# A stick-breaking scan that reads its factors from PSUM, and a planner that knows of a shared port

## The chip, the cores and the metric

The kernel runs on one core of a Trainium2 chip. Its time is the device time of one launch in microseconds (us); the median of three runs is given. Five engines work on it at once, each in its own order: TensorE (PE, with its weight loads PEld), VectorE (DVE), ScalarE (ACT), GpSimd (POOL) and SyncE (SP), which issues the DMAs. The program divides PSUM, into which PE writes its products, into eight banks of 512 fp32 columns.

## The reference

One decoder layer in fp32, 2048 tokens of width 1024. A combined projection feeds two head groups of eight heads: latent attention with softmax (MLA), and stick-breaking attention. Both outputs are normalised, concatenated and projected; a SwiGLU feed-forward network follows. The change is in the second group:

```python
z = jnp.einsum("bhqd,bhkd->bhqk", qb, kf) * scale
strict = k_pos[None, :] < q_pos[:, None]
log_beta = jax.nn.log_sigmoid(z)
log_one_minus = jnp.where(strict, jax.nn.log_sigmoid(-z), 0.0)
suffix = lax.cumsum(log_one_minus, axis=3, reverse=True) - log_one_minus
a = jnp.where(strict, jnp.exp(log_beta + suffix), 0.0)
o = jnp.einsum("bhqk,bhkd->bhqd", a, vf)
```

So the weight of key s is beta[s] times the product of 1 - beta over the keys between s and the query.

## The kernel before

**Precision.** Operands of large products are split into a high part in fp32r and the rest, a low part (`split_w` line 518, `split_ps` line 509): ACT writes the high part (`whi`, `ph`), DVE subtracts it (`wlo`, `pl`), and PE makes three products out of them (`mm3`).

**Stages.** `ORDER` (line 86) lists, for four blocks of 512 tokens, the projection P, the attention A, and the feed-forward parts F. All of their instructions go into one `Plan`. Attention runs from about 200 to 1900 us, beside projections and the first feed-forward products; afterwards PE has dense products alone.

**Attention.** For each head, block and stretch of 1024 keys there is a `Unit`; `step` (line 754) makes four rows of 128 queries. `sb_row` (line 636) cuts the keys into pieces of up to 512, last piece first. For each piece PE makes the scores in a PSUM tile `ps_s` (two products), ACT writes 1 - beta into an SBUF tile `nb` and beta into `p` (line 647), and DVE scans `nb` backwards into `tb` (lines 657 to 665): each step multiplies the running value with the next factor. A masked scan of 128 columns comes first in the piece on the diagonal. POOL then multiplies p by tb (line 666). The value that the scan ends with starts the next piece. `mix` (line 585) takes pairs of rows: PE transposes p into a PSUM tile `pt`, ACT and DVE split it into `ph` and `pl`, and PE multiplies v with both into `ot`.

**Buffers.** The PSUM banks are shared: two for scores (`S_B`), two for transposes (`TP_B`), one for `ot` (`O_B`), the rest for dense accumulators (`ps_gu`, `ps_d`, `ps_o` and others). In SBUF there are two `nb` and two `tb` (`NT_BUFS`), and six p (`P_BUFS`).

**What sets the order.** `Plan.order` (line 282) is a list scheduler that runs while the program is built. Each instruction has a cost (`price`, line 237), each pair of engines a handover (`HOP`), and each pool its buffers. At each moment an engine takes the ready instruction of lowest rank, then of lowest index. What comes out is each engine's fixed order; on the chip an engine executes strictly in it and waits where an operand is late. A product into `ot` needs the one recorded before it on the same columns. `issue` (line 436) writes all instructions, so they all carry line 450 in the profile.

Of the kernel before, what the change touches and what calls it, by code (L numbers as in the profile page):

```python
# [12 lines left out]
F32 = mybir.dt.float32  # L13
F32R = mybir.dt.float32r
I32 = mybir.dt.int32
AF = mybir.ActivationFunctionType
ALU = mybir.AluOpType
# [4 lines left out]
P = 128  # L22
# [37 lines left out]
NT_BUFS = 2  # L60
SWAP_SPAN = 0.5
AHEAD = 10
RT_BUFS = 3
SLACK = 0.0
DMA_ISSUE = 500.0
DMA_RATE = 300.0
DMA_DONE = 910.0
# [114 lines left out]
class Plan:  # L182
# [21 lines left out]
    def record(self, engine, method, args, kwargs):  # L204
        t = Task()
        t.engine, t.method, t.args, t.kwargs = engine, method, args, kwargs
        t.index, t.key = len(self.tasks), (self.rank, len(self.tasks))
        views = [(i, a) for i, a in enumerate(args)] + list(kwargs.items())
        views = [(k, v) for k, v in views if isinstance(v, View)]
        first = 0 if "out" not in kwargs else "out"  # L210
        t.out = next((v for k, v in views if k == first), None)
        t.needs, t.then, t.bases = set(), [], []
        for k, v in views:
            write = k in (first, "accum_out")
            base, region = v.base, v.region or v.base.whole
            if base not in t.bases:
                t.bases.append(base)
            for old, oreg, owrite in base.seen:
                if k == first and engine == "tensor" == old.engine and kwargs.get("start"):
                    t.needs.add(old.index)  # L220
                if (write or owrite) and old is not t and all(a < d and c < b for (a, b), (c, d) in zip(region, oreg)):
                    t.needs.add(old.index)
            if write:
                base.seen = [s for s in base.seen if s[0] is t or not all(a <= c and d <= b for (a, b), (c, d) in
                                                                           zip(region, s[1]))]
            base.seen.append((t, region, write))
        for b in t.bases:
            b.uses += 1
        t.table, t.cost, t.tail = self.price(t)
        if engine != "tensor" and any(b.pool.managed and b.pool.psum for b in t.bases):  # L230
            boost = ACC_FIRST if any(b.tag == "acc" for b in t.bases) else ATT_FIRST
            t.key = (self.rank - boost, t.index)
        elif engine != "tensor" and self.dense:
            t.key = (self.rank - DENSE_FIRST, t.index)
        self.tasks.append(t)
# [46 lines left out]
    def order(self):  # L282
        tasks = self.tasks
# [18 lines left out]
        ready = {e: [] for e in self.ENGINES}  # L302
        parked = {}
        free_at = {e: 0.0 for e in self.ENGINES}
        wire = 0.0
        events = []
        seq = itertools.count()
# [38 lines left out]
        now = 0.0  # L346
        result = []
        while len(result) < len(tasks) or events:
            moved = True
            while moved:  # L350
                moved = False
                for e in self.ENGINES:
                    while ready[e] and free_at[e] <= now:
                        key, i = heapq.heappop(ready[e])
# [5 lines left out]
                        if e == "scalar" and t.table and table and t.table != table:  # L360
                            held = []
                            while ready[e] and len(held) < 24:
                                k2, j = heapq.heappop(ready[e])
                                u = tasks[j]
                                if (not u.table or u.table == table) and not u.opens and k2[0] <= key[0] + SWAP_SPAN:
                                    held.append((key, i))
                                    t, key, i = u, k2, j
                                    break
                                held.append((k2, j))
                            for h in held:  # L370
                                heapq.heappush(ready[e], h)
                        cost = t.cost
                        if e == "scalar" and t.table and t.table != table:
                            cost += 1280
                            table = t.table
# [78 lines left out]
def layer(ctx, tc, x, positions, inv_freq, norm_mix, w_in, q_latent_norm, w_uq,  # L454
# [73 lines left out]
    with ExitStack() as s:  # L528
# [56 lines left out]
        def mix(ot, r0, rows, v, c0):  # L585

            at = [{k0 // P + i: p[:, i * P:(i + 1) * P] for p, k0, n in row for i in range(n // P)} for row in rows]
            js = sorted(at[1])
            for ja in js[::2]:
                pair = [(j, [r for r in range(2) if j in at[r]]) for j in js if ja <= j < ja + 2]  # L590
                n = sum(len(rs) for _, rs in pair) * P
                pt = tp.tile([P, TB], F32, tag="tp", name="pt")
                x = 0
                for j, rs in pair:
                    for r in rs:
                        plan.tensor.transpose(pt[:, x:x + P], at[r][j], ident)
                        x += P
                ph = wk.tile([P, TB], F32R, tag="ph", name="ph", bufs=PH_BUFS)
                pl = wk.tile([P, TB], F32R, tag="pl", name="pl", bufs=PH_BUFS)
                split_ps(pt[:, :n], ph[:, :n], pl[:, :n])  # L600
                x = 0
                for j, rs in pair:
                    w = len(rs) * P
                    o0 = (r0 + rs[0]) * P
                    for half in (ph, pl):
                        plan.tensor.matmul(ot[:, o0:o0 + w], lhsT=v[:, j - c0 // P, :], rhs=half[:, x:x + w],
                                           start=j == js[0] and half is ph, stop=j == js[-1] and half is pl)
                    x += w

        def mla_row(r, b, c0, k, q, mx, sm):  # L610
            rs_ = slice(r * P, (r + 1) * P)
# [24 lines left out]
        def sb_row(r, b, c0, k, q, carry, carry_out):  # L636
# [4 lines left out]
            for k0, n, last in reversed(pieces(b, r, c0)):  # L641
                p = pp.tile([P, 512], F32, tag="p", name="p")
                ps = sp.tile([P, 512], F32, tag="s", name="ps_s")
                scores(ps, k0, n, False, lhs)
                nb = wk.tile([P, 512], F32, tag="nb", name="nb", bufs=NT_BUFS)
                tb = wk.tile([P, 513], F32, tag="tb", name="tb", bufs=NT_BUFS)
                plan.scalar.activation(nb[:, :n], ps[:, :n], AF.Sigmoid, scale=-SC_S)
                plan.scalar.activation(p[:, :n], ps[:, :n], AF.Sigmoid, scale=SC_S)
                if after is None:
                    plan.vector.memset(tb[:, n:n + 1], 1.0)  # L650
                else:
                    plan.vector.tensor_copy(tb[:, n:n + 1], after)
                rev = nb[:, :n][:, ::-1]
                if last:
                    d = n - P
                    plan.gpsimd.tensor_tensor(out=p[:, d:n], in0=p[:, d:n], in1=below, op=ALU.mult)
                    plan.vector.tensor_tensor_scan(tb[:, d:n][:, ::-1], rev[:, :P], beyond[:, ::-1], tb[:, n:n + 1],
                                                 op0=ALU.mult, op1=ALU.max)
                    if d:
                        rest_ = rev[:, P:]  # L660
                        plan.vector.tensor_tensor_scan(tb[:, :d][:, ::-1], rest_, rest_, tb[:, d:d + 1],
                                                     op0=ALU.mult, op1=ALU.bypass)
                else:
                    plan.vector.tensor_tensor_scan(tb[:, :n][:, ::-1], rev, rev, tb[:, n:n + 1],
                                                 op0=ALU.mult, op1=ALU.bypass)
                plan.gpsimd.tensor_tensor(out=p[:, :n], in0=p[:, :n], in1=tb[:, 1:n + 1], op=ALU.mult)
                after = tb[:, 0:1]
# [841 lines left out]
```

## Time and profile before

| | us |
|---|---|
| median of 3 runs | 3097.14 (3095.7 to 3098.21) |
| the profiled execution | 3101.35 |
| its span, first to last instruction | 3099.6 |
| PE busy (share of the span) | 2994.7 (97%) |
| PE weight loads busy | 2540.0 (82%) |
| DVE busy | 2432.5 (78%) |
| ACT busy | 1799.4 (58%) |
| POOL busy | 604.9 (20%) |
| granted TensorE clock, mean | 0.991 |

A busy share is an average over stages. Matmuls are pipelined: the profile shows each with some 0.39 us while one follows the other every 0.23 us, so a busy PE is not PE at its peak. Most lines of the profile carry the same line number, so instructions are told apart by what they write and read: `tb<-nb,tb` is the scan, `p<-p,tb` POOL's multiply.

### The profile page before, as it was taken

The numbers are of one execution on the slowest core, as the hardware profiler recorded it, in microseconds if no ns is written. First come the engines' busy times: TensorE is split into PE (matmuls) and PEld (weight loads), VectorE is DVE, ScalarE is ACT, GpSimd is POOL, SyncE is SP. The second block draws the span as 40 slices with busy tenths as digits, with TensorE's granted clock in tenths as the row PEclk, the third lists the DMA queues.
The fourth block names the chain that finished last, engine by engine and source line by source line (L and its number), as shares of the span: only waits on it lengthen the run. The fifth ranks groups of instructions, "written<-read, shape, count | busy, mean of one in ns | idle before, by whom it ended". The sixth has DMA issues, their size and how long they took to land.

```text
span 3099.6 us, 47762 instructions
## 1 busy us (share of the span) xinstructions
PE 2994.7 (97%) x16372; PEld 2540.0 (82%) x16372; DVE 2432.5 (78%) x4927; ACT 1799.4 (58%) x3864; POOL 604.9 (20%) x619
## 2 busy tenths in 40 slices
PE   8899999999999999999999999999999999999998
PEld 7889888888888888888887878888888788888887
DVE  6568888988998988888989797665666877776777
ACT  5457867777787776766776765454434333323323
POOL 0002322222231322422223140100012200100011
PEclk9999999999999999999999999999999999999999
DMA  6988866566656334343333334565543311211212
GB/s 197 268 262 236 260 205 181 150 207 202 194 170 192 112 119 122 104 140 116 120 113 102 98 112 133 177 184 176 170 129 116 129 55 44 66 41 55 62 48 82
DMA packets 403433, 437.79 MB, mean 141 GB/s; under 512 B 76875, under 2 KB 296054, under 8 KB 403190
## 3 DMA queue, kind: packets, MB, share of 16 engines
q1 hardware_dynamic: 403190, 434.74, 46.2%
q8 instruction: 129, 2.11, 0.3%
q14 instruction: 114, 0.93, 0.1%
HBM read 350.78 MB, written 83.89 MB: 140 GB/s over the span
## 4 chain that ended last, share of the span: by engine, by line
PE 68%; DVE 18%; DMA 5%; issue 4%; ACT 3%; SPq 0%; POOL 0%; DVEq 0%; POOLq 0%; ACTq 0%
PE ps_m L450 14%; PE ps_d L450 14%; PE ps_gu L450 11%; DVE tb L450 9%; PE ps_s L450 6%; PE ot L450 5%; PE ps_o L450 4%; PE pt L450 4%; PE ps_q L450 3%; DVE pl L450 3%; DVE wlo L450 2%; PE ps_v L450 2%; PE ps_lat L450 2%; DVE acc L450 1%; PE ps_t L450 1%
## 5 line engine op out<-in xcount | busy, mean ns | idle before, releaser
L450 ACT ACTIVATE whi<-raw 128x512 fp32r<-128x512 f32 (+1 forms) x726 | 448.8, 627 | 578.3 <-PE ps_d L450 205.1
L450 DVE TENSOR_TENSOR wlo<-raw,whi 128x512 fp32r<-128x512 f32 (+1 forms) x726 | 526.0, 733 | 195.6 <-ACT whi L450 190.2
L450 ACT ACTIVATE ph<-pt 128x512 fp32r<-128x512 f32 (+1 forms) x576 | 322.6, 581 | 146.1 <-PE pt L450 139.8
L450 POOL TENSOR_TENSOR p<-p,tb 128x512 f32<-128x512 f32 (+3 forms) x320 | 333.4, 1044 | 343.9 <-DVE tb L450 270.8
L450 PE MATMUL ps_s<-k,q 128*128 128x512 f32 (+3 forms) x1280 | 384.1, 377 | 15.4 <-DMA k<-d_mk 7.2
L450 DVE TENSOR_TENSOR pl<-pt,ph 128x512 fp32r<-128x512 f32 (+1 forms) x576 | 368.3, 649 | 21.2 <-ACT ph L450 19.4
L450 PE MATMUL pt<-ident,p 128*128 128x128 f32 x2176 | 362.6, 275 | 9.6 <-POOL p L450 4.5
L450 DVE TENSOR_TENSOR_SCAN tb<-nb,tb 128x512 f32<-128x512 f32 (+3 forms) x288 | 356.8, 1240 | 4.9
L450 PE MATMUL ps_m<-fop,whi 128*128 128x512 f32 (+1 forms) x1254 | 357.3, 373 | 0.0
L450 PE MATMUL ot<-pl,v 128*128 128x256 f32 (+1 forms) x1152 | 315.5, 303 | 28.3 <-DVE pl L450 19.4
L450 PE MATMUL ot<-ph,v 128*128 128x256 f32 (+1 forms) x1152 | 314.6, 284 | 3.8 <-ACT ph L450 3.1
L450 DVE TENSOR_TENSOR acc<-acc,ps_d 128x512 f32<-128x512 f32 x352 | 236.5, 681 | 87.1 <-PE ps_d L450 86.9
L450 PEld LDWEIGHTS ot<-pl,v 128*128 128x128 f32 x1152 | 218.3, 189 | 88.7 <-DVE pl L450 55.0
L450 PE MATMUL ps_d<-whi,hh 128*128 128x512 f32 x704 | 278.2, 396 | 7.9 <-ACT hh L450 6.2
L450 PEld LDWEIGHTS pt<-ident,p 128*128 128x128 f32 x2176 | 258.3, 141 | 32.3 <-POOL p L450 10.0
L450 PE MATMUL ps_gu<-tl,whi 128*128 128x512 f32 x704 | 280.8, 399 | 0.0
L450 PE MATMUL ps_gu<-th,whi 128*128 128x512 f32 x704 | 280.6, 399 | 0.0
L450 PE MATMUL ps_gu<-th,wlo 128*128 128x512 f32 x704 | 280.3, 398 | 0.0
L450 PE MATMUL ps_d<-wlo,hh 128*128 128x512 f32 x704 | 277.1, 394 | 0.0
L450 PE MATMUL ps_d<-whi,hl 128*128 128x512 f32 x704 | 273.9, 395 | 0.0
L450 PEld LDWEIGHTS ps_m<-fop,whi 128*128 128x128 f32 x1254 | 226.1, 188 | 45.1
L450 PEld LDWEIGHTS ps_s<-k,q 128*128 128x128 f32 x1280 | 221.2, 190 | 45.4 <-DMA k<-d_mk 7.6
(222 smaller groups left out, 6262.6 us busy)
## 6 DMA issues: line engine op xcount, KB each, us to landing
raw<-in_w_gate SPq DMA_DIRECT2D x66, 512.0 KB, 4.6
raw<-in_w_up SPq DMA_DIRECT2D x66, 512.0 KB, 4.3
raw<-in_w_down SPq DMA_DIRECT2D x66, 512.0 KB, 4.2
raw<-in_w_o SPq DMA_DIRECT2D x64, 512.0 KB, 4.3
raw<-in_w_in SPq DMA_DIRECT2D x48, 512.0 KB, 6.0
q<-d_mq SPq DMA_DIRECT2D x64, 256.0 KB, 5.8
q<-d_sbq SPq DMA_DIRECT2D x64, 256.0 KB, 5.2
k<-d_mk SPq DMA_DIRECT2D x32, 512.0 KB, 6.1
```

What stands on the lines that cost most here:

```text
L450: getattr(getattr(nc, t.engine), t.method)(*args, **kwargs)
```

## The change

It has three parts. In `sb_row` ACT writes p first and then 1 - beta over the scores in their own PSUM tile; `nb` is gone from there, and the scan takes its factors from PSUM. The scan's second operand, which the operation `bypass` ignores, is now p. In `mix` the products of the high parts of both key blocks come ahead of those of the low parts. In `Plan`, instructions that take two SBUF inputs on DVE, and POOL's tensor_tensor other than pow, are marked as users of one port: the planner lets one run at a time, and where the port stays taken for over 100 ns it looks for another ready instruction on that engine.

```diff
--- before.py
+++ after.py
@@ -62,6 +62,7 @@
 AHEAD = 10
 RT_BUFS = 3
 SLACK = 0.0
+PORT_WAIT = 100.0
 DMA_ISSUE = 500.0
 DMA_RATE = 300.0
 DMA_DONE = 910.0
@@ -227,6 +228,11 @@
         for b in t.bases:
             b.uses += 1
         t.table, t.cost, t.tail = self.price(t)
+
+        t.port = (engine == "gpsimd" and method == "tensor_tensor" and kwargs.get("op") != ALU.pow
+                  or engine == "vector" and method in ("tensor_tensor", "scalar_tensor_tensor", "tensor_tensor_scan")
+                  and not any(isinstance(a, View) and a.base.pool.psum for a in
+                              (kwargs.get("in0"), kwargs.get("in1"), *(args[1:3] if "scan" in method else ()))))
         if engine != "tensor" and any(b.pool.managed and b.pool.psum for b in t.bases):
             boost = ACC_FIRST if any(b.tag == "acc" for b in t.bases) else ATT_FIRST
             t.key = (self.rank - boost, t.index)
@@ -302,6 +308,7 @@
         ready = {e: [] for e in self.ENGINES}
         parked = {}
         free_at = {e: 0.0 for e in self.ENGINES}
+        port_free = 0.0
         wire = 0.0
         events = []
         seq = itertools.count()
@@ -369,7 +376,22 @@
                                 held.append((k2, j))
                             for h in held:
                                 heapq.heappush(ready[e], h)
+                        if t.port and port_free > now + PORT_WAIT:
+                            held = [(key, i)]
+                            while ready[e] and len(held) < 24:
+                                k2, j = heapq.heappop(ready[e])
+                                u = tasks[j]
+                                if not u.port and all(closed(b) is None for b in u.opens):
+                                    t, key, i = u, k2, j
+                                    break
+                                held.append((k2, j))
+                            for h in held:
+                                if h[1] != i:
+                                    heapq.heappush(ready[e], h)
                         cost = t.cost
+                        if t.port:
+                            cost += max(0.0, port_free - now)
+                            port_free = now + cost
                         if e == "scalar" and t.table and t.table != table:
                             cost += 1280
                             table = t.table
@@ -598,14 +620,14 @@
                 ph = wk.tile([P, TB], F32R, tag="ph", name="ph", bufs=PH_BUFS)
                 pl = wk.tile([P, TB], F32R, tag="pl", name="pl", bufs=PH_BUFS)
                 split_ps(pt[:, :n], ph[:, :n], pl[:, :n])
-                x = 0
-                for j, rs in pair:
-                    w = len(rs) * P
-                    o0 = (r0 + rs[0]) * P
-                    for half in (ph, pl):
+                for half in (ph, pl):
+                    x = 0
+                    for j, rs in pair:
+                        w = len(rs) * P
+                        o0 = (r0 + rs[0]) * P
                         plan.tensor.matmul(ot[:, o0:o0 + w], lhsT=v[:, j - c0 // P, :], rhs=half[:, x:x + w],
                                            start=j == js[0] and half is ph, stop=j == js[-1] and half is pl)
-                    x += w
+                        x += w
 
         def mla_row(r, b, c0, k, q, mx, sm):
             rs_ = slice(r * P, (r + 1) * P)
@@ -642,26 +664,24 @@
                 p = pp.tile([P, 512], F32, tag="p", name="p")
                 ps = sp.tile([P, 512], F32, tag="s", name="ps_s")
                 scores(ps, k0, n, False, lhs)
-                nb = wk.tile([P, 512], F32, tag="nb", name="nb", bufs=NT_BUFS)
                 tb = wk.tile([P, 513], F32, tag="tb", name="tb", bufs=NT_BUFS)
-                plan.scalar.activation(nb[:, :n], ps[:, :n], AF.Sigmoid, scale=-SC_S)
                 plan.scalar.activation(p[:, :n], ps[:, :n], AF.Sigmoid, scale=SC_S)
+                plan.scalar.activation(ps[:, :n], ps[:, :n], AF.Sigmoid, scale=-SC_S)
                 if after is None:
                     plan.vector.memset(tb[:, n:n + 1], 1.0)
                 else:
                     plan.vector.tensor_copy(tb[:, n:n + 1], after)
-                rev = nb[:, :n][:, ::-1]
+                rev, other = ps[:, :n][:, ::-1], p[:, :n][:, ::-1]
                 if last:
                     d = n - P
                     plan.gpsimd.tensor_tensor(out=p[:, d:n], in0=p[:, d:n], in1=below, op=ALU.mult)
                     plan.vector.tensor_tensor_scan(tb[:, d:n][:, ::-1], rev[:, :P], beyond[:, ::-1], tb[:, n:n + 1],
                                                  op0=ALU.mult, op1=ALU.max)
                     if d:
-                        rest_ = rev[:, P:]
-                        plan.vector.tensor_tensor_scan(tb[:, :d][:, ::-1], rest_, rest_, tb[:, d:d + 1],
+                        plan.vector.tensor_tensor_scan(tb[:, :d][:, ::-1], rev[:, P:], other[:, P:], tb[:, d:d + 1],
                                                      op0=ALU.mult, op1=ALU.bypass)
                 else:
-                    plan.vector.tensor_tensor_scan(tb[:, :n][:, ::-1], rev, rev, tb[:, n:n + 1],
+                    plan.vector.tensor_tensor_scan(tb[:, :n][:, ::-1], rev, other, tb[:, n:n + 1],
                                                  op0=ALU.mult, op1=ALU.bypass)
                 plan.gpsimd.tensor_tensor(out=p[:, :n], in0=p[:, :n], in1=tb[:, 1:n + 1], op=ALU.mult)
                 after = tb[:, 0:1]
```

The instructions of each engine are the same in number, but for ACT's table loads; the order is new from the first attention block on. On ACT, around the scores of one head of the second attention block (tile 16475 before; 16648 and 16667 are scores of the same unit now; `os`, `po` belong to the unit before, `whi` and `hh` to dense work). Before:

```order
L450 ACTIVATE p_16487<-ps_s_16475 128x512
L450 ACTIVATE nb_16497<-ps_s_16436 128x512
L450 ACTIVATE whi_16503<-raw_16150 128x512
L450 ACTIVATE nb_16516<-ps_s_16475 128x512
L450 ACTIVATE p_16523<-ps_s_16510 128x512
L450 ACTIVATE os_16532<-ot_16445 128x512
L450 ACTIVATE nb_16553<-ps_s_16510 128x512
L450 ACTIVATE po_16559<-po_16543 128x256
```

and in the change:

```order
L472 ACTIVATE p_16653<-ps_s_16648 128x512
L472 ACTIVATE ps_s_16648<-ps_s_16648 128x512
L472 ACTIVATE p_16675<-ps_s_16667 128x512
L472 ACTIVATE os_16683<-ot_16582 128x512
L472 ACTIVATE ps_s_16667<-ps_s_16667 128x512
L472 ACTIVATE po_16699<-po_16692 128x256
L472 ACTIVATE p_16707<-ps_s_16689 128x512
L472 ACTIVATE ph_16713<-pt_16701 128x512
```

The passes to `nb` have become passes in place, each behind the p of its tile.

On PE at the same place, the products into `ot` (`ps_gu`, `ps_d` are dense products, `ps_s` scores). Before:

```order
L450 MATMUL ot_16445<-ph_16471,v_16121 128x256
L450 MATMUL ps_gu_16429<-th_13517,wlo_16170 128x512
L450 MATMUL ps_gu_16429<-th_13527,whi_16075 128x512
L450 MATMUL ps_gu_16429<-tl_13545,whi_16075 128x512
L450 MATMUL ps_gu_16429<-th_13527,wlo_16170 128x512
L450 MATMUL ps_gu_16429<-th_13549,whi_16075 128x512
L450 MATMUL ps_gu_16429<-tl_13562,whi_16075 128x512
L450 MATMUL ps_gu_16429<-th_13549,wlo_16170 128x512
L450 MATMUL ot_16445<-pl_16494,v_16121 128x256
L450 MATMUL ot_16445<-ph_16471,v_16121 128x256
L450 MATMUL ot_16445<-pl_16494,v_16121 128x256
L450 MATMUL ot_16445<-ph_16479,v_16121 128x256
```

and in the change, in one piece with the scores that follow:

```order
L472 MATMUL ot_16582<-ph_16623,v_16245 128x256 x2
L472 MATMUL ps_d_16627<-whi_16340,hl_16309 128x512
L472 MATMUL ps_d_16637<-whi_16288,hh_16301 128x512
L472 MATMUL ps_d_16637<-wlo_16311,hh_16301 128x512
L472 MATMUL ps_d_16637<-whi_16288,hl_16309 128x512
L472 MATMUL ps_s_16648<-k_16373,q0_15905 128x512
L472 MATMUL ps_s_16648<-k_16373,q1_15921 128x512
L472 MATMUL ps_d_16616<-whi_16418,hh_16639 128x512
L472 MATMUL ot_16582<-pl_16644,v_16245 128x256 x2
L472 MATMUL ot_16582<-ph_16633,v_16245 128x256
L472 MATMUL ot_16582<-ph_16633,v_16245 128x128
L472 MATMUL ps_d_16616<-wlo_16435,hh_16639 128x512
```

Both `ph` products of a pair of key blocks now stand together, then dense products and scores, then both `pl` products; before, the second `ph` stood between the two `pl`. The same order goes on, up to the scores that take over the bank of tile 16648:

```order
L472 MATMUL ps_d_16627<-whi_16482,hh_16639 128x512
L472 MATMUL ps_d_16627<-wlo_16540,hh_16639 128x512
L472 MATMUL ps_s_16667<-k_16373,q0_15905 128x512
L472 MATMUL ps_s_16667<-k_16373,q1_15921 128x512
L472 MATMUL ps_d_16637<-whi_16418,hh_16639 128x512
L472 MATMUL ot_16582<-pl_16664,v_16245 128x256
L472 MATMUL ot_16582<-pl_16664,v_16245 128x128
L472 MATMUL ps_d_16616<-whi_16418,hl_16658 128x512
L472 MATMUL ps_d_16627<-whi_16482,hl_16658 128x512
L472 MATMUL ps_d_16637<-wlo_16435,hh_16639 128x512
L472 MATMUL ps_d_16637<-whi_16418,hl_16658 128x512
L472 MATMUL ps_s_16689<-k_16373,q0_15905 128x512
```

Of the score tiles two are in use at a time, so the products into 16689 wait for the scan of 16648.

## Rows read from the trace of the kernel before

**Rows 1.** The page: engines busy; then groups of instructions, busy us, mean ns, idle before.
```profile
PE 2994.7 (97%) x16372; PEld 2540.0 (82%) x16372; DVE 2432.5 (78%) x4927; ACT 1799.4 (58%) x3864; POOL 604.9 (20%) x619
...
L450 DVE TENSOR_TENSOR_SCAN tb<-nb,tb 128x512 f32<-128x512 f32 (+3 forms) x288 | 356.8, 1240 | 4.9
```

**Rows 2.** The windows: the attention stretch, busy us of each engine (instructions), clock, DMA.
```profile
200.00:1870.00 1670.00, 1605.57 (x9841) 1378.89 (x9841) 1456.04 (x3204) 1215.14 (x2722) 463.30 (x493) 0.99 0.52 158
```

**Rows 3.** The chain in order of time: start us, us, what, how many.
```profile
110.08 2.88 PE ps_v L450 x24
...
2088.64 21.81 PE ps_gu L450 x96
```

**Rows 4.** The chain of the stretch 200 to 1870 us, shares by line.
```profile
by line: DVE tb L450 16.6%; PE ps_s L450 11.2%; PE ot L450 9.1%; PE pt L450 7.5%; issue 7.5%; PE ps_gu L450 6.9%; DVE pl L450 5.2%; PE ps_d L450 3.6%; DVE wlo L450 2.9%; PE ps_v L450 2.8%; PE ps_o L450 2.4%; PE ps_q L450 2.2%; ACT p L450 1.
```

**Rows 5.** The tile tb: DVE instructions, ns min/median/max, first and last start.
```profile
L450 DVE TENSOR_TENSOR_SCAN tb<-nb,tb x288: 469/1272/2317, 223.7 to 1861.6; 128x512 f32<-128x512 f32 x96, 128x128 f32<-128x128 f32 x16, 128x384 f32<-128x384 f32 x16, 128x256 f32<-128x256 f32 x16
...
L450 DVE TENSOR_TENSOR_SCAN tb<-nb,tb,beyond x128: 453/485/1492, 222.0 to 1830.2; 128x128 f32<-128x128 f32 x128
```

**Rows 6.** The timeline of DVE: start us, us, instruction.
```profile
1174.47 0.53 DVE L450 TENSOR_TENSOR pl<-pt,ph 128x384 fp32r<-128x384 f32 x1
...
1176.08 1.93 DVE L450 TENSOR_TENSOR_SCAN tb<-nb,tb 128x512 f32<-128x512 f32 x1
...
1178.16 2.17 DVE L450 TENSOR_TENSOR_SCAN tb<-nb,tb 128x512 f32<-128x512 f32 x1
...
1186.18 1.27 DVE L450 TENSOR_TENSOR_SCAN tb<-nb,tb 128x512 f32<-128x512 f32 x1
```

**Rows 7.** The timeline of POOL in the same stretch.
```profile
1173.42 3.52 POOL L450 TENSOR_TENSOR p<-p,tb 128x512 f32<-128x512 f32 x2
1178.16 1.09 POOL L450 TENSOR_TENSOR p<-p,tb 128x512 f32<-128x512 f32 x1 [1.23 <-DVE tb L450]
...
1185.16 1.09 POOL L450 TENSOR_TENSOR p<-p,tb 128x512 f32<-128x512 f32 x1 [1.34 <-DVE tb L450]
```

**Rows 8.** DVE by form, 200 to 1870 us: busy us, mean ns, idle before.
```profile
L450 DVE TENSOR_TENSOR pl<-pt,ph 128x512 fp32r<-128x512 f32 x433 | 290.3, 678 | 18.3 <-ACT ph L450 16.7
L450 DVE TENSOR_TENSOR_SCAN tb<-nb,tb 128x512 f32<-128x512 f32 x192 | 281.4, 1465 | 4.1
L450 DVE TENSOR_TENSOR wlo<-raw,whi 128x512 fp32r<-128x512 f32 x248 | 193.9, 790 | 6.1 <-ACT whi L450 4.4 <-PE ps_q L450 1.0 <-ACT p L450 0.5
...
L450 DVE TENSOR_TENSOR_SCAN tb<-nb,tb,beyond 128x128 f32<-128x128 f32 x128 | 78.9, 623 | 13.4 <-ACT nb L450 10.7
L450 DVE TENSOR_TENSOR pl<-pt,ph 128x384 fp32r<-128x384 f32 x125 | 68.3, 546 | 1.7 <-ACT ph L450 1.4
...
L450 DVE TENSOR_TENSOR_SCAN tb<-nb,tb 128x384 f32<-128x384 f32 x32 | 34.3, 1071 | 0.2
```

**Rows 9.** The timeline of ACT: in brackets the wait and who ended it.
```profile
1178.11 0.60 ACT L450 ACTIVATE nb<-ps_s 128x512 f32<-128x512 f32 x1 [1.81 <-DVE tb L450]
...
1180.37 0.60 ACT L450 ACTIVATE nb<-ps_s 128x512 f32<-128x512 f32 x1 [1.38 <-DVE tb L450]
```

**Rows 10.** The timeline of PE.
```profile
1181.50 0.39 PE L450 MATMUL ot<-ph,v 128*128 128x256 f32 x1 [0.62 <-ACT ph L450]
```

**Rows 11.** POOL and ACT by form, whole run: busy us, mean ns, idle before.
```profile
L450 POOL TENSOR_TENSOR p<-p,tb 128x512 f32<-128x512 f32 x224 | 261.7, 1170 | 270.7 <-DVE tb L450 201.3 <-ACT p L450 16.9 <-ACT ph L450 15.9
...
L450 ACT ACTIVATE nb<-ps_s 128x512 f32<-128x512 f32 x224 | 136.4, 609 | 55.5 <-DVE tb L450 51.8 <-PE pt L450 1.4 <-PE ps_s L450 0.6
...
L450 ACT ACT_TABLE_LOAD x58 | 74.4, 1283 | 1.8 <-PEq L1498 0.8
```

**Rows 12.** The tile wlo: DVE, ns min/median/max.
```profile
L450 DVE TENSOR_TENSOR wlo<-raw,whi x726: 560/686/1785, 14.5 to 3068.2; 128x512 fp32r<-128x512 f32 x166, 128x416 fp32r<-128x416 f32 x16
```

**Rows 13.** The waits, 200 to 1870 us: us in total, times, longest us.
```profile
ACT nb L450 <- DVE tb L450: 63.4, 84, 2.3
...
PEld ot L450 <- DVE pl L450: 55.0, 111, 1.4
```

## The prediction

> **What bounds the kernel now.** I read the engines' busy time first, then the same over the stretch in which attention runs, then the chain of waits of that stretch, then the instructions behind its largest entry. TensorE is busy 97% of the span [rows 1], but that mixes two things. From 200 to 1870 us, while the four attention blocks run, PE is busy 1605.57 of 1670 us, DVE 1456.04, ACT 1215.14 and POOL 463.30 [rows 2]. PE's weight loads, which cannot look busy by pipelining, fill only 1378.89 us of it. After 1870 us dense products run back to back: 96 products of one kind take 21.81 us, 0.227 us each [rows 3]. So PE loses its time in attention, and what it waits for there is what a change can win.
>
> The chain of that stretch names it: its largest entry is `DVE tb`, the stick-breaking scan, 16.6%, or 277 us; `DVE pl` has 5.2% and `DVE wlo` 2.9% (48 us) [rows 4]. The scan is in no PE wait by itself: it makes DVE late, DVE is in order, and ACT, POOL and PE wait in turn.
>
> Why it is late is in its durations. Alone, a scan over 512 columns takes 1.27 us (the row at 1186.18, with POOL's multiply over 0.07 us later, and the median of the group, 1272 ns); the one at 1176.08 took 1.93 and the one at 1178.16 took 2.17 [rows 5, 6]. Beside these two, POOL was multiplying p by tb [rows 7]: at 1178.16 both began together, POOL needed its normal 1.09 us and the scan 0.90 us more than alone. The two multiplies from 1173.42 took 3.52 us where two alone take 2.18. So scan and multiply hold each other up. `pl` does not suffer: at 1174.47 it took 0.53 us inside POOL's 3.52, no more than its group's mean of 546 ns for 384 columns [rows 6, 8]. The difference is the source: `pl` takes one input from PSUM and one from SBUF; the scan, `wlo` and the multiply take both from SBUF.
>
> The damage is then passed on: ACT stood 1.81 and 1.38 us before `nb`, because only two nb buffers exist and DVE had not released one [rows 9], and PE stood 0.62 us before a product for which ACT's `ph` was late [rows 10].
>
> **The change part by part.** *1. The scan reads 1 - beta in PSUM.* Its second operand becomes p, which `bypass` ignores, so one input is in PSUM, like `pl`'s. By the forms: 192 scans of 512 columns, mean 1465 against 1272 alone, lose 37.1 us; 128 masked scans of 128 columns, mean 623 against a median of 485, lose 17.7 us; 32 of 384 columns, mean 1071 against some 1010 (on the line through 485 and 1272), lose 2.0 us [rows 5, 8]. Together 57 us, 13% of the group's 435.7 us (356.8 + 78.9) [rows 1, 8]. The chain holds 277 of these 435.7 us, 64%, so 36 us of the 57 are on the path: **-36 us**. Ends: 0, if the scan stretches as before, and -57, if every stretch delayed the end. I take the chain's share, since the excess sits where POOL and DVE are both pressed. POOL's own excess (224 x (1.17 - 1.09) = 18 us [rows 7, 11]) I cost at nothing: POOL is busy 463 of 1670 us, and that cover holds as long as a score row's product with tb is not the next thing PE transposes.
>
> The price of a scan out of PSUM does not stand in the trace. Nearest rows: `pl` of 512 columns, one input in PSUM, mean 678 ns, and the median of `wlo`, both inputs in SBUF, 686 ns [rows 8, 12]. I take no difference. The ends are -8 ns and +193 ns (1465 - 1272), at which part 1 would bring nothing; that is rival C.
>
> [...]
>
> *2. ScalarE writes into the scores.* 320 passes to `nb` (609 ns for 512 columns) become 320 passes in place [rows 11], priced alike. No row shows a pass that reads and writes one bank; from above I allow it twice the time, 136 us more for the full ones, which would take ACT from 1215 to some 1350 of 1670 us, still less than DVE has. The order turns round: p first, 1 - beta second, so the scan can start one pass (0.6 us) later than before. Hidden as long as DVE has a backlog, which its 1456 of 1670 us imply. The wait for nb buffers, 84 times and 63.4 us on ACT [rows 13], goes: no nb is left.
>
> *3. The score tile stays until the scan is done.* This is the added wait. There are two score tiles; until now one came free when ACT had read it twice. Behind the waiting scores product stand all of PE's other products, in order. From below it costs nothing, if the planner's order has enough other products in between; from above PE takes over undiluted what ACT waits today, 63.4 us. In the order shown, from the last product of score tile 16648 to the first of 16689 stand 9 `ps_d` and 2 `ps_s` products of 0.227 us and 6 `ot` products of at most 0.12 us (24 `ps_v` of the same 256 columns take 2.88) [rows 3]: 3.2 us. Against that stand p, 1 - beta and the scan: 0.61 + 0.61 + 1.27 = 2.5 us, without handovers and DVE's queue. The cover is there but thin; I take one eighth of the upper end: **+8 us**.
>
> *4. Low parts last in `mix`.* Nothing is added. PE waits 111 times, 55.0 us, for `pl` before loading v [rows 13]. The order now has the second `ph` product (0.12 us) ahead of the low ones where it stood behind. At most 111 x 0.12 = 13 us, at least 0, since the planner already put dense products there: **-6 us**.
>
> *5. The planner knows of the shared port.* It keeps multiplies of POOL and DVE's SBUF-to-SBUF work apart when another instruction is ready. What this touches after part 1 is `wlo`: 248 x (790 - 686) = 26 us in the stretch, of which the chain holds 25% (48 of 194 us), 6 us [rows 4, 8, 12]; half of them: **-3 us**. Everything is reordered, DMA issues too: instructions and bytes stay the same on every queue. ACT's table loads fall from 58 to 52 by the count over the order; 6 x 1.28 us [rows 11] lie on ACT beside other work and I count none of it.
>
> Sum: -36 + 8 - 6 - 3 = **-37 us**. The profiled execution took 3101.35 us (span 3099.6 us), 0.14% above the median of the runs, 3097.14. So 3064 beside the profile, and **3060 us** as the median.
>
> **The rivals.**
> *A, slower: PE waits for the score tile.* If DVE stays backlogged, each tile is kept by a scan that has not begun, and PE, unlike ACT, has everything behind it. For it: two tiles only, p now ahead of 1 - beta, 3.2 us of cover for 2.5 us of passes. Against: the planner knows of it and spaces the scores. Price: the whole 63.4 us in place of 8, so -45 + 63 = +18: 3115 us. It decides once the extra wait is over 45/320 = 0.14 us per stick-breaking tile.
> *B, no difference: the wait moves on.* DVE gets through earlier, but PE's order now has the same gaps before `ph` and p, so that only parts 4 and 5 remain and part 3 eats them: 3097 us. For it: the chain's PE entries are latency (transpose, copy, subtract, product), which a faster scan does not shorten. Against: the long ACT stalls stand right at stretched scans [rows 6, 9].
> *C, the change does not do what it says: the scan stretches still*, because p is in SBUF as second operand, or a reversed read in PSUM is as slow as the gain. Then part 1 is 0: -1, 3096 us; by the forms a difference would show in the scan's durations at once.
> *D, more than I sum.* ACT's order is no longer stopped by nb, and all of DVE's 57 + 26 us come back, with the upper 13 us of part 4 and nothing lost in part 3: -96, 3001 us.
>
> **How the numbers follow.** My forecast 0.50, A 0.17, B 0.11, C 0.06, D 0.16. A measurement of this kernel can tell 0.2%, 6 us, from no change. Faster: the forecast, D, and a quarter of B and C: 0.70. Same: most of B and C, 0.11. Slower: A and a little of C, 0.19. The forecast's own range, between its parts' ends for parts 3 to 5, is 3025 to 3090. To leave out no more than 2 in 10 it must reach most of D and most of A: 3010 to 3112.
>
> **What would show it.** Right: scans of 512 columns at about 1.27 us beside POOL, and those of 128 at 0.48; the multiply at 1.09; ACT without a wait for `tb`; `DVE tb` well under 277 us in the chain of the attention stretch; PE's waits for `pl` below 55 us. Wrong in part 3: waits of the weight load or product `ps_s` for `tb`, tens of microseconds. Wrong in part 1: scans over 1.4 us in the mean, or a floor above 1.3 us. The forecast falls if attention's last product comes later by more than the dense work that was moved ahead of it.

## The result, and the profile after

The changed kernel takes **3042.66 us** (median, 3041.96 to 3046.05), the kernel before 3096.42: a ratio of 0.983 [0.9813, 0.9847], or 53.8 us less. The profiled execution took 3046.05 us, its span 3044.3 us. Forecast were 3060 us and a range of 3010 to 3112: the right side, inside the range, 17 us too slow.

The page's busy time and, below it, the attention stretch by windows (busy us of each engine with its instructions, clock, DMA share, GB/s), against [rows 1, 2]:

```profile
PE 2966.1 (97%) x16372; PEld 2544.5 (84%) x16372; DVE 2382.7 (78%) x4927; ACT 1786.1 (59%) x3858; POOL 574.8 (19%) x619
```
```profile
200.00:1870.00 1670.00, 1633.04 (x10069) 1430.09 (x10068) 1428.29 (x3248) 1225.07 (x2767) 435.77 (x494) 0.99 0.55 165
```

PE does the same 16372 products, but gets 228 more of them done inside these 1670 us (10069 against 9841). At 0.227 us per dense product [rows 3] they are 52 us, an estimate close to the gain. It takes products of different size as one, however, and is no measure in general: with the port alone (experiment 4) the stretch holds 9822, 19 fewer than before, and that kernel is 22 us faster. A cut at the end of attention shows more. The tile `po` holds PE's last products of attention (first and last start), and the windows run from there to the end. Before, and then the change:

```profile
L450 PE MATMUL po<-ident,os x384: 270/272/330, 243.0 to 1911.8; 128*128 128x128 f32 x192
...
1912.10:3100.00 1187.90, 1168.99 (x5328) 966.64 (x5326) 820.89 (x1318) 441.32 (x800) 130.61 (x105) 0.99 0.34 103
```
```profile
L472 PE MATMUL po<-ident,os x384: 270/272/329, 240.2 to 1942.6; 128*128 128x128 f32 x192
...
1942.90:3045.00 1102.10, 1085.02 (x4943) 897.26 (x4941) 774.46 (x1226) 402.39 (x723) 116.60 (x94) 0.99 0.31 97
```

Attention ends 31 us later than before, but 4943 products are left behind it where 5328 were, at 0.223 us each in both (1187.5 and 1101.4 us to the end of the span). So 385 products, 86 us of work, have moved ahead of that end; less the 31 us this is 55 us, the difference of the two spans. The time was won where the prediction looked for it; the products behind attention got no faster.

The chain of 200 to 1870 us by line, against [rows 4]:

```profile
by line: PE ps_s L472 17.0%; PE ps_gu L472 14.7%; PE ot L472 13.7%; PE pt L472 11.9%; PE ps_d L472 7.3%; PE ps_o L472 5.2%; PE ps_q L472 4.2%; DVE tb L472 2.4%; PE ps_v L472 2.3%; PE po L472 2.1%; issue 2.0%; PE ps_lat L472 1.3%; DVE pl L47
```

`DVE tb` fell from 16.6% to 2.4%; nine of the ten largest entries are now PE's own work. The groups by form over the whole run (busy us, mean ns) and, below, the tile tb (ns min/median/max), against [rows 5, 8, 11, 12]:

```profile
L472 DVE TENSOR_TENSOR wlo<-raw,whi 128x512 fp32r<-128x512 f32 x662 | 486.2, 741 | 179.4 <-ACT whi L472 172.4 <-PE ps_gu L472 2.5 <-PE ps_mk L472 2.0
...
L472 POOL TENSOR_TENSOR p<-p,tb 128x512 f32<-128x512 f32 x224 | 259.0, 1156 | 264.6 <-DVE tb L472 252.8 <-ACT ps_s L472 4.6 <-PE ps_d L472 2.2
L472 DVE TENSOR_TENSOR_SCAN tb<-ps_s,tb,p 128x512 f32<-128x512 f32 x192 | 244.5, 1274 | 6.0 <-ACT ps_s L472 3.1 <-DVE tb L472 0.5
...
L472 ACT ACTIVATE ps_s<-ps_s 128x512 f32<-128x512 f32 x224 | 134.5, 603 | 0.0
...
L472 DVE TENSOR_TENSOR_SCAN tb<-ps_s,tb,beyond 128x128 f32<-128x128 f32 x128 | 60.0, 474 | 25.2 <-ACT ps_s L472 24.3
```
```profile
L472 DVE TENSOR_TENSOR_SCAN tb<-ps_s,tb,p x288: 465/1270/1285, 222.8 to 1880.6; 128x512 f32<-128x512 f32 x96, 128x128 f32<-128x128 f32 x16, 128x384 f32<-128x384 f32 x16, 128x256 f32<-128x256 f32 x16
```

The longest of all scans takes 1285 ns, where it was 2317. A full one takes 1274 ns from PSUM, and took 1272 from SBUF when alone. ScalarE's pass in place takes 603 ns, `nb` took 609. `wlo`, on the other hand, still averages 741 ns (746 before, in a group of the same 662): the planner's new rule did not make it shorter.

The waits of the stretch (us in all, times, longest), against [rows 13]:

```profile
DVE tb L472 <- ACT ps_s L472: 26.9, 29, 3.6
...
PEld ot L472 <- ACT ph L472: 23.9, 47, 2.6
...
PEld ot L472 <- DVE pl L472: 6.3, 15, 1.4
...
PEld ps_s L472 <- DVE tb L472: 4.3, 8, 1.1
PE ps_s L472 <- DVE tb L472: 2.6, 5, 0.9
```

PE's weight load waits 6.3 us for `pl` where it waited 55.0. The wait for the held score tile is there: 4.3 us on the load and 2.6 on the product. ACT's wait for nb is gone with nb, and DVE waits 26.9 us for 1 - beta, which now comes second. The load's wait for `ph` doubled (11.9 before, one of the lines of that view that rows 13 left out). The products into `ot` themselves, behind their loads, waited 19.4 us for `pl` and 3.1 for `ph` before, and now 2.3 and 12.6.

### The profile page after: what moved, and what is told of

It is laid out like the page before. It is cut to its first block, busy times and chain, and to the rows that moved or that the text cites. A ratio compares the mean times of both kernels' runs of the same rounds, so it can differ in the third digit from the quotient of the medians.

```text
span 3044.3 us, 47607 instructions
## 1 busy us (share of the span) xinstructions
PE 2966.1 (97%) x16372; PEld 2544.5 (84%) x16372; DVE 2382.7 (78%) x4927; ACT 1786.1 (59%) x3858; POOL 574.8 (19%) x619
## 3 DMA queue, kind: packets, MB, share of 16 engines
q8 instruction: 129, 2.11, 0.3%
## 4 chain that ended last, share of the span: by engine, by line
PE 85%; DVE 5%; DMA 5%; ACT 3%; issue 1%; SPq 0%; POOL 0%; ACTq 0%; POOLq 0%; DVEq 0%
PE ps_gu L472 15%; PE ps_d L472 15%; PE ps_m L472 14%; PE ps_s L472 10%; PE ot L472 8%; PE pt L472 7%; PE ps_o L472 5%; PE ps_q L472 5%; PE ps_v L472 2%; PE ps_lat L472 2%; DVE tb L472 1%; PE po L472 1%; PE ps_t L472 1%; DVE acc L472 1%; DMA raw<-in_w_in 1%
## 5 line engine op out<-in xcount | busy, mean ns | idle before, releaser
L472 ACT ACTIVATE ph<-pt 128x512 fp32r<-128x512 f32 (+1 forms) x576 | 315.8, 577 | 137.0 <-PE pt L472 123.0
L472 POOL TENSOR_TENSOR p<-p,tb 128x512 f32<-128x512 f32 (+3 forms) x320 | 326.6, 1021 | 351.4 <-DVE tb L472 337.0
L472 DVE TENSOR_TENSOR_SCAN tb<-ps_s,tb,p 128x512 f32<-128x512 f32 (+3 forms) x288 | 315.4, 1096 | 6.6 <-ACT ps_s L472 3.1
L472 PE MATMUL ot<-pl,v 128*128 128x256 f32 (+1 forms) x1152 | 245.9, 293 | 3.2 <-DVE pl L472 2.3
L472 PE MATMUL ot<-ph,v 128*128 128x256 f32 (+1 forms) x1152 | 232.9, 283 | 12.9 <-ACT ph L472 12.6
L472 PEld LDWEIGHTS ot<-pl,v 128*128 128x128 f32 x1152 | 201.7, 192 | 38.6 <-DVE pl L472 6.5
```

The costliest lines, as they stand in the source:

```text
L472: getattr(getattr(nc, t.engine), t.method)(*args, **kwargs)
```

## The experiments

The theory: the scan held up by POOL over SBUF is what costs PE time, and the two other parts add little. Its rivals: the order that the planner makes is what counts (new waits, a rule, luck), not the scan. Twelve kernels ran; each is compared with the kernel before on the same chip (3098.9, 3097.8 and 3098.6 us in the three batches).

**1. The same order, with the scan's factors in SBUF again.** The plan of the changed kernel is made and kept instruction by instruction; only at issue ScalarE's second pass writes a tile nb instead of the score tile, and the scan reads nb; with p its two inputs are in SBUF again.

```diff
-            args = [real(a) for a in t.args]
+            swap = getattr(t, "swap", {})
+            args = [real(swap.get(i, a)) for i, a in enumerate(t.args)]
...
                 plan.scalar.activation(ps[:, :n], ps[:, :n], AF.Sigmoid, scale=-SC_S)
+                plan.tasks[-1].swap = {0: nb[:, :n]}
...
+                    plan.tasks[-1].swap = {1: nb[:, :n][:, ::-1]}
```

> The changed kernel with every engine's order kept, instruction by instruction; ScalarE writes 1 - beta into an SBUF tile and the scan reads it there, so that the scan has two SBUF inputs again (score tiles come free earlier than in the change, nothing else differs). If the gain came from the scan no longer being held up by POOL: scans of 512 columns are back at a mean of 1.4 to 1.5 us, some 57 us of DVE time return, and the time rises from 3043 to 3080 or more. Rival, the gain came from the new order: the scans stretch, but the time stays within 10 us of 3043.

3077.7 us, ratio 0.9935 [0.9923, 0.9948]: **35 us more than the change in the same order** (33 if each is set against the kernel before that ran beside it). That is 2 us short of the 3080 that was expected, and far above the 3053 up to which the order alone would have explained the gain. Since the order is the same, the same instructions can be laid beside each other. DVE and then POOL of the changed kernel (timeline: start us, us, what, and in brackets the wait before it):

```profile
788.14 1.28 DVE L472 TENSOR_TENSOR_SCAN tb<-ps_s,tb,p 128x512 f32<-128x512 f32 x1
...
792.17 1.27 DVE L472 TENSOR_TENSOR_SCAN tb<-ps_s,tb,p 128x512 f32<-128x512 f32 x1
```
```profile
788.06 1.12 POOL L472 TENSOR_TENSOR p<-p,tb 128x512 f32<-128x512 f32 x1 [1.21 <-DVE tb L472]
...
792.08 1.11 POOL L472 TENSOR_TENSOR p<-p,tb 128x512 f32<-128x512 f32 x1 [0.69 <-DVE tb L472]
```

The same two of each in experiment 1:

```profile
791.85 2.11 DVE L473 TENSOR_TENSOR_SCAN tb<-nb,tb,p 128x512 f32<-128x512 f32 x1
...
796.70 2.11 DVE L473 TENSOR_TENSOR_SCAN tb<-nb,tb,p 128x512 f32<-128x512 f32 x1
```
```profile
791.75 1.12 POOL L473 TENSOR_TENSOR p<-p,tb 128x512 f32<-128x512 f32 x1 [1.22 <-DVE tb L473]
...
796.62 1.12 POOL L473 TENSOR_TENSOR p<-p,tb 128x512 f32<-128x512 f32 x1 [0.69 <-DVE tb L473]
```

The scan that starts 0.1 us behind POOL's multiply takes 2.11 us out of SBUF and 1.27 out of PSUM; POOL, which was first, takes the same in both. Over all, in experiment 1, DVE's busy time (its page), the waits of the stretch, and the end of attention with what comes behind it:

```profile
PE 2979.0 (97%) x16372; PEld 2539.0 (83%) x16372; DVE 2440.0 (79%) x4927; ACT 1787.1 (58%) x3858; POOL 606.6 (20%) x619
```
```profile
PEld ot L473 <- DVE pl L473: 20.9, 49, 1.4
...
PEld ot L473 <- DVE tb L473: 12.3, 23, 1.5
...
ACT nb L473 <- DVE tb L473: 0.5, 1, 0.5
```
```profile
L473 PE MATMUL po<-ident,os x384: 270/272/421, 243.0 to 1976.9; 128*128 128x128 f32 x192
...
1977.20:3076.20 1099.00, 1083.40 (x4943) 896.27 (x4941) 774.33 (x1226) 402.73 (x723) 116.89 (x94) 1.00 0.31 97
```

2440.0 against 2382.7: 57.3 us of DVE time, of which 35 come out at the end, 61% (57% by the 33). They come out inside attention: it ends 34 us later than in the change, and the same 4943 products behind it take 1099 us against 1101. The two nb buffers are not the cause, since ACT waits only 0.5 us in all for one to come free. This experiment takes back part 1 of the prediction and part 3 as well, since the score tile is free again when ACT has read it: no wait of `ps_s` for `tb` is in its list.

**2 to 4. Each part alone.** Three edits of the changed kernel, each undoing one part, give all combinations. "Port" is the planner's word here: the runs show how long scan and multiply take beside each other (experiment 1), not what in the chip holds the scan up. No port (P):

```diff
+PORT = False
...
-        t.port = (engine == "gpsimd" and method == "tensor_tensor" and kwargs.get("op") != ALU.pow
+        t.port = PORT and (engine == "gpsimd" and method == "tensor_tensor" and kwargs.get("op") != ALU.pow
```

No low parts last (M), the loop over the key blocks outside again:

```diff
-                for half in (ph, pl):
-                    x = 0
-                    for j, rs in pair:
...
+                x = 0
+                for j, rs in pair:
...
+                    for half in (ph, pl):
```

No scan from PSUM (S), the lines of `sb_row` as before:

```diff
+                nb = wk.tile([P, 512], F32, tag="nb", name="nb", bufs=NT_BUFS)
...
+                plan.scalar.activation(nb[:, :n], ps[:, :n], AF.Sigmoid, scale=-SC_S)
...
-                plan.scalar.activation(ps[:, :n], ps[:, :n], AF.Sigmoid, scale=-SC_S)
...
-                rev, other = ps[:, :n][:, ::-1], p[:, :n][:, ::-1]
+                rev = nb[:, :n][:, ::-1]
```

The scan from PSUM alone (P and M undone):

> The kernel before with the scan in PSUM alone: no port in the planner, low parts as before. Step 1 and 3 of the prediction alone, -36 + 8: about 3068. Scans at 1.27 us, no wait of ScalarE for tb. Rival (the planner's knowledge of the port is what counts): 3085 or more.

3064.62 us, 0.9889 [0.9874, 0.9904]: 34 us less than before, as much as experiment 1 took back, in another order. Its `ps_s` waits for `tb` are 8.0 us on the load and 5.3 on the product.

The low parts last alone (P and S undone):

> The kernel before with the low parts' products last alone. Step 4 alone: -6, between -13 and 0, about 3090; PE's waits for pl fall from 55 us by some 13. Rival (the fall of the waits for pl from 55.0 to 6.3 us in the change is this part's doing): 3055 to 3065.

3093.82 us, 0.9985 [0.9976, 0.9994]: 5 us less. The load's wait for `pl` falls by 4.6 us, from 55.0 to 50.4, where some 13 were expected.

The port alone (M and S undone):

> The kernel before with the planner's knowledge of the port alone; the scan still reads nb in SBUF and counts as a user of the port. Scans should then stretch less because POOL and DVE are kept apart in the plan: mean of 512 columns 1.30 to 1.40 us in place of 1.465. By step 5 the time falls by little, 3075 to 3095, since the port is taken in turn instead of at once. Rival (planning for the port is the gain): 3060 or less.

3076.56 us, 0.9929 [0.9916, 0.9943]: 22 us less. Two of its groups over the whole run, and its waits of the stretch:

```profile
L472 DVE TENSOR_TENSOR wlo<-raw,whi 128x512 fp32r<-128x512 f32 x662 | 502.5, 767 | 165.0 <-ACT whi L472 156.1 <-PE ps_gu L472 2.2 <-PE ps_mk L472 2.0
...
L472 DVE TENSOR_TENSOR_SCAN tb<-nb,tb 128x512 f32<-128x512 f32 x192 | 265.6, 1383 | 2.1
```
```profile
ACT nb L472 <- DVE tb L472: 29.1, 35, 3.2
...
PEld ot L472 <- DVE pl L472: 6.3, 16, 1.5
```

The scans lose 16 us of their excess (192 x 82 ns), `wlo` gains none (767 ns). What falls further are the waits: 6.3 us for `pl` where the kernel before has 55.0, and 29.1 us of ACT for a free nb where it has 63.4. No run prices these one by one.

**5 to 7. Each pair.** Scan and low parts last (P undone):

> The change without the planner's knowledge of the port (scan in PSUM and low parts last remain). If parts add up as they measured alone (-34 and -5): about 3058, 15 above the change. If planning for the port is worth its whole 22 us also without the scan's contention: 3064. If it is worth only what step 5 said once the scan is out of the way (3 us): 3046.

3061.61 us, 0.9889 [0.9875, 0.9903]: 19 us above the change, nearer to the 22 of the port alone than to the 3 of the prediction.

Scan and port (M undone):

> The change with the low parts' products in the old place. Step 4 says 3 to 13 us are lost: 3046 to 3056. Rival (once DVE is in time, the place of the low products is worth nothing, since the planner fills the gap either way): 3040 to 3046, with PE's waits for pl still below 15 us.

3064.43 us, 0.9897 [0.9883, 0.9912]: 22 us above the change, above both ranges that were expected (3046 to 3056, 3040 to 3046) and far more than the low parts gave alone; and the port added nothing to the scan alone, though the load's wait for `pl` fell from 33.4 to 9.3 us between the two.

Low parts last and port (S undone):

> The change with the scan reading nb in SBUF, planned as such: the planner knows of the port and of two nb buffers. If parts add up: -22 - 5, about 3070. If the planner knows of the contention anyway and only pays it in DVE time, 3065 to 3078; ScalarE's wait for tb, 63.4 us before, stays below 35. Rival (planning and scan are worth the same us twice): 3050 or less.

3080.56 us, 0.9948 [0.9936, 0.996]: 4 us above the port alone and above the 3078 that was expected at most. The parts do not add: 34, 5 and 22 us make 61 alone, no pair beats 37, and all three make 54.

**8. The port counted, but not avoided.** The planner still adds the wait for the port to an instruction's time, but takes no other instruction in its place.

```diff
-PORT_WAIT = 100.0
+PORT_WAIT = 1e9
```

> The change with PORT_WAIT so large that the planner never looks for another instruction: it only reckons the time that the port makes an instruction wait. If the planner's gain comes from knowing when things will be late, and placing what waits for them later, the time stays within 8 us of 3043 and wlo beside POOL is as stretched as in the change (mean of all 512-column ones 741 ns). If it comes from keeping the two engines apart: 3055 or more, with wlo and the multiply longer.

3060.62 us, 0.9879 [0.9864, 0.9894]: 18 us above the change, and within 1 us of experiment 5, without the port. Its waits of the stretch:

```profile
PEld ps_s L472 <- DVE tb L472: 11.2, 13, 2.6
...
PE ps_s L472 <- DVE tb L472: 8.7, 10, 2.2
...
PEld ot L472 <- DVE pl L472: 4.3, 14, 0.6
```

The two signs that were set point apart. `wlo` averages 748 ns and the multiply 1153, as in the changed kernel (741 and 1156), but the time is that of the other side, on which keeping the two engines apart is what counts. The wait for `pl` is short: for that it is enough that the planner counts the port's time. The short wait brought no time here. The waits for the held score tile are longer than in the change (4.3 and 2.6 us there), so some of the 18 us may lie in them; for the rest these rows show no cause but that the order is another one. That raised the question of what an order is worth by chance.

**9 to 12. Other plans of the same programs.** The planner counts 5 ns more for each handover between engines. Nothing else changes, yet the whole order falls out differently.

```diff
-SLACK = 0.0
+SLACK = 5.0
```

The kernel before:

> The kernel before, but the planner counts 5 ns more for each handover between engines (SLACK 5 instead of 0). Instructions and buffers are the same; the whole order falls out differently. Theory 1 (each part of the change has an effect of its own, and the three help each other): the order found by chance matters little, so 3098 us, within 5. Theory 2 (each plan carries some 10 to 20 us of luck either way): 3078 to 3118, and off 3098 by more than 8.

3136.82 us, 1.012 [1.0102, 1.0137]: **38 us slower by another order alone**, and above the 3118 that was expected at most. Its scans stretch more, 1516 ns in the mean where 1465 stood, some 10 us of DVE time in all; what makes the rest is not shown:

```profile
L450 DVE TENSOR_TENSOR_SCAN tb<-nb,tb 128x512 f32<-128x512 f32 x192 | 291.1, 1516 | 4.2
```

The changed kernel:

> The changed kernel with the same 5 ns. Theory 1: 3043 us, within 5, some 55 below e9. Theory 2: between 3045 and 3070, because the 3043 was a lucky draw; the scan in PSUM alone guarantees some 34 us against e9.

3067.91 us (3054.84 to 3072.16), 0.9892 [0.9873, 0.991]: 25 us above the change, inside the 3045 to 3070 of theory 2, and 69 below experiment 9.

The changed kernel without the low parts last (M undone):

> The changed kernel without the low parts last, with the same 5 ns. Theory 1: as without the 5 ns, 22 us above e10, about 3064. Theory 2: no fixed distance from e10; within 10 us of it, or on the other side of it.

3069.64 us, 0.9906 [0.9891, 0.9921]: 2 us above experiment 10, less than the executions of that one differ by (17 us), where 22 stood. So the 22 hang on the order.

The changed kernel without the port (P undone):

> The changed kernel without the planner's knowledge of the port, with the same 5 ns. Theory 1: as without the 5 ns, 19 us above e10, about 3062. Theory 2: no fixed distance from e10; within 10 us of it, or on the other side of it.

3088.12 us, 0.9964 [0.995, 0.9977]: 20 us above experiment 10, as the 19 between experiment 5 and the change. So the size of a single comparison can come from the order, as theory 2 has it. For the port beside both others two plans agree, as theory 1 has it, but that is one agreement and no proof.

All together, in us (medians; the wait is the weight load's for `pl` in the attention stretch):

| kernel | time | wait | with 5 ns: time | wait |
|---|---|---|---|---|
| before | 3098 | 55.0 | 3136.8 | 39.5 |
| low parts last | 3093.8 | 50.4 | | |
| port | 3076.6 | 6.3 | | |
| low parts last, port | 3080.6 | 6.6 | | |
| scan | 3064.6 | 33.4 | | |
| scan, low parts last | 3061.6 | 27.6 | 3088.1 | 20.6 |
| scan, port | 3064.4 | 9.3 | 3069.6 | 5.8 |
| all: the change | 3042.7 | 6.3 | 3067.9 | 5.4 |
| the change, factors in SBUF, same order | 3077.7 | 20.9 | | |

Each part by its pairs of rows: the scan -34, -32, -12 and -38, in the mean -29; the low parts -5, -3, +4, -22 and -2, in the mean -6; the port -22, 0, -13, -19 and -20, in the mean -15. The same program in another plan: +38, +27, +5 and +25. All four moved the same way, 24 us in the mean, so the 5 ns may well make a worse plan of every program, and this is not shown to be mere chance; from that mean the single ones differ by up to 19 us. A difference between two plans can therefore carry some 20 us that no part of the edit explains; only experiment 1, which keeps the order, is free of it. The wait for `pl` is steadier than the time: in all five pairs the port's part takes it to between 5 and 10 us. It does not go with the time, though: the port alone has the 6.3 us of the change and is 34 us slower.

## Why the prediction was right, step by step

- **The bound: right, but for two of its signs.** Weight loads can look busy too: in the trace before, loads of 0.19 us start 0.11 us apart, at 1181.50 and 1181.61 us. Behind attention, too, they fill only 81% of the time (966.64 of 1187.90 us), against 83% in the attention stretch, so they do not tell where PE loses time. Nor is the scan in no PE wait: the load of v waits 13.7 us for `tb` before, 1.4 in the change and 12.3 in experiment 1.
- **1 (scan in PSUM, -36): right in mechanism and near in size.** Scans went to 1274 and 474 ns as forecast. Forecast was that 64% of 57 us come out at the end; experiment 1 shows 57.3 us of DVE time and 35 us at the end, 61%. That includes part 3, so parts 1 and 3 together, forecast -28, are -35 (or -33) by experiment 1 and -34 by experiment 2.
- **The price of PSUM: none, as taken from the row for `pl`.** 1274 ns against 1272.
- **2 (ScalarE in place): right in its price.** 603 ns where 609 was taken. The later second pass is not wholly hidden: DVE now waits 26.9 us for it, where 10.7 us stood before for nb in the same view; no run prices that wait by itself.
- **3 (score tile held, +8): the wait came and is small; no run prices it alone.** The waits of `ps_s` for `tb`, the load's and the product's, add up to 6.9 us, longest 1.1, and to 19.9 us in experiment 8. Rival A needed over 45 us of them and falls.
- **4 (low parts last, -6): -5 alone**, and -6 in the mean of five pairs, which lie between -22 and +4. No pair is free of the order, so none proves that the part differs from nothing. The wait that it was to shorten fell by 4.6 us alone.
- **5 (the planner knows the port, -3): the step that failed, in size and in what it touches.** It said "What this touches after part 1 is `wlo`" and counted half of the 6 us of that group's excess that lie on the chain. `wlo` is unchanged (741 ns). The part is worth between 0 and -22 us in five pairs, -15 in the mean. What the step overlooked: a planner that counts how late DVE will be also orders PE anew. In all five pairs the wait for `pl` becomes short, and experiment 8 shows it short with the counting alone. That wait was read and given to part 4 instead, with at most 13 us; the port's part takes 49 us of it alone. By which path the part saves time stays open: in experiment 8, and with scan and port, the wait is short and the time no better than without the port.
- **Rival B happened in part.** The load's wait for `ph` rose by 12 us while that for `pl` fell by 49; the product's own rose by 9.5 and fell by 17.
- **Rivals C and D.** C falls with the first scan. D asked for all 57 us at the end, the upper end of part 4 and 26 us of `wlo`; none of these came. The result lies between forecast and D above all because of part 5 (-15 in the mean for -3), and then of parts 1 and 3 (-34 for -28). How far a good draw of the order helped is not known: the same change in another plan gains 31 us on the kernel before, and 69 on that kernel in its other plan.
- **The range and the other signs.** The forecast's own range, 3025 to 3090, does not follow from the ends that it names: -36 with 0 to 63 for part 3, -13 to 0 for part 4 and -6 to 0 for part 5 makes 3042 to 3124. The multiply did not come to 1.09 us (1156 ns in the mean). Attention's last product did come later, by 31 us, but 86 us of work were moved ahead of it, so the forecast did not fall by that.

What stays open: how much of the change's last 18 us, against experiments 5, 6 and 8, is its own, and how the port's part saves time. Two plans per program are too few to say.

## What to carry to other kernels

Where DVE and POOL both read two operands from SBUF, look for operations that take longer beside each other than alone (here 2.11 us against 1.27). Having the producer write one operand into PSUM, in place over what it has just read, cured it here at no price in the operation (1274 ns against 1272); the PSUM tile then stays taken for longer (PE's waits of `ps_s` for `tb` were 6.9 us). When an edit passes through a planner, test it once with the order held, and draw several other plans by a small change of a planning cost: here one such change alone moved the time by 5 to 38 us, as much as most edits, and each time upward. A short wait in a planned order is no proof of time won: here counting how late an engine will be was enough for the short wait, and the time did not follow it.

## What the runs showed of the hardware that was not expected

- With the order held, taking one operand from SBUF to PSUM changed a scan beside a multiply from 2.11 to 1.27 us and POOL's multiply not at all (1.11 to 1.12 us in both). In the first pair the multiply began 0.10 us earlier and lost nothing; the scan, which began with 1.02 us of the multiply still to run, lost 0.84 us.
- The multiply is not freed altogether: it averages 1156 ns with the scan in PSUM, 1170 before, against 1.09 us alone. Most of the prediction's 18 us of excess on POOL (224 x (1.156 - 1.09) = 15 us) are still there: at 271.10 us, for one, it took 1.50 us beside a `wlo`.
- A change of 5 ns in one planning constant, with the same instructions, made the kernel before 38 us slower, as much as the 35 us that the scan was worth with the order held.
